# A hybrid decoder step: the next chunk's gate products ahead of the down products, and a decode maximum that reads PSUM

## The chip, the cores and the metric

The kernel runs on one core of one Trainium2 chip. The metric is the device time of one execution, in microseconds (us). A core has TensorE (PE; its weight loads are shown as PEld), VectorE (DVE), ScalarE (ACT), GpSimd (POOL) and SyncE (SP), each with an instruction queue of its own, and 16 DMA engines that move data between the chip's main memory and its working memory (SBUF). Products of TensorE land in PSUM, eight banks of 512 float32 values per partition.

## The reference

One layer of a decoder serves 512 prompt tokens and 8 samples of 4 new tokens each, 544 tokens in all, with shared weights. The width is 1024.

```python
h = h + 0.5 * rmsnorm(swiglu(rmsnorm(h, norm_g[0]), wg[0], wu[0], wd[0]), norm_g[1])
m, c_kv, k_r, s_fin = mixer(rmsnorm(h, norm_g[2]), ...)
h = h + rmsnorm(m, norm_g[3])
h = h + 0.5 * rmsnorm(swiglu(rmsnorm(h, norm_g[4]), wg[1], wu[1], wd[1]), norm_g[5])
```

`swiglu(x)` is `(silu(x @ wg) * (x @ wu)) @ wd`, with 2816 inner columns, which the kernel walks as 22 tiles of 128. The mixer has two groups of heads: a gated linear recurrence, and latent attention with a softmax over keys. For the samples the keys are 4096 cached rows each, gathered through a page table (256 latent and 64 rotary values per row). For every sample the attention computes

```python
s = (ql . c_kv + qr . k_rope) * scale       # 4 heads x 4 tokens = 16 rows against the keys
p = softmax(s);  o = p . c_kv
```

All data are float32. A product of two float32 operands is split into a high and a low part each and takes three TensorE products (high x high, high x low, low x high).

## The kernel before, in words

**Stages.** First the first FFN on all tokens (to about 390 us), then the mixer's projections, the recurrence and the prompt's attention (to about 700 us). Then two pieces of work run side by side: the samples' attention, called decode, and the second FFN on the first 256 prompt tokens (half 0). Then the output projection and the second FFN for the other 288 tokens (half 1) close the run.

**The FFN** is the generator `ffn` (line 324). Its 22 inner tiles are cut in chunks, `FCH[1]` = 6, 6, 5 and 5 tiles. For each tile f it loads the gate weight, multiplies (`gemm_q`, line 269, for half 0; `gemm` for half 1), loads the up weight, multiplies, and then scales the gate product by the row norm `r2` (line 350), forms its sigmoid in three ScalarE instructions (`sigmoid`, line 319), multiplies twice on VectorE (lines 352 and 353), and splits the result in a high part `hh` (ScalarE) and a low part `hl` (VectorE) (`split`, line 169). At the end of a chunk eight down products over the chunk's tiles follow. With `fine` the first two of them are `gemm_2` (line 280): both first take all but the chunk's last tile, and the last tile's products come at the end. `fine` is set only for the second FFN on half 0.

`weight` (line 232) loads a weight through SP's queue into one of five buffers `wraw`, casts it to the high part `wh` on ScalarE (line 250) and subtracts for the low part `wl` on VectorE (line 251).

**Quanta.** With `fine` the generator yields after every four of a product's eight inner slices, that is after 12 TensorE products of 256 columns, and after each down product (18 or 15 products). One such piece is called a quantum here.

**Decode** works on 16 halves (8 samples, two halves of 2048 keys each), class `Half`. It proceeds in steps `st` = 0 to 4 for each n. In the steps of one n, four halves are at work at different places:

- `turn`: VectorE transposes gathered keys to `kh` (line 1367), two instructions a step.
- `score` (line 1370): 80 small float32 products into two PSUM banks `self.s[0]` and `self.s[1]`, 48 of them at st = 2 and 32 at st = 4 (`RUNS`); the trace shows each as two records, 96 and 64. After the last, ScalarE copies the first bank and VectorE the second to `self.e` in SBUF (line 1385), and one VectorE reduction gives the maximum per row (`self.mx`, tile mxh, line 1387).
- `peak` (line 1389), at st = `PEAK` = 1 of the next n: a product with the identity turns and spreads the maximum (tile pm, line 1391), VectorE reduces it per query (line 1393) and forms the bias (line 1396), ScalarE takes the exponentials of `self.e` in place with their sum (line 1397), VectorE transposes them (line 1399), and 12 ScalarE and 4 VectorE copies spread them in `pbuf` (line 1403).
- `value` (line 1405), at st = 4 of that n: 16 products with the gathered rows, 32 records.
- `gathered` (line 1417), at st = 1 one n later: the output is turned and copied.

The two score banks have the tag "ps" with two buffers, so the next half's first scores wait until both are free.

**Order.** The main loop takes one decode step, and then as many quanta of the FFN's generator as keep 100 of them spread evenly over 94 steps. Each engine's instructions are put in order ahead of the run by the framework's planner: the order of the program is the priority, and an instruction that is not ready by the planner's own estimates lets later ones pass. So the order on an engine is near the program's, and not the same everywhere. `tc.issue_after` holds some instructions behind a named one; the change touches none of these. Waits between engines follow from the data and the buffers.

Of the kernel before, what the change touches and what calls it, by code (L numbers as in the profile page):

```python
# [8 lines left out]
F32 = mybir.dt.float32  # L9
# [8 lines left out]
P = 128  # L18
# [45 lines left out]
NDEC = 100  # L64
JS = ((8, 9), (0, 1), (2, 3), (4, 5), (6, 7))
KHB = 4
PEAK = 1
RUNS = {2: (0, 1, 2), 4: (3, 4)}
LEVELS = (32, 16, 8, 4, 2, 1)
CH = 64  # L70
# [40 lines left out]
def hybrid_step_kernel(  # L111
# [150 lines left out]
    def gemm(wt, act_):  # L262
        wh, wl, kt = wt
        acc = ps("acc", "acc")
        n = act_[0].shape[-1]
        mm3(acc[:, :n], [((wh[:, k], wl[:, k]), (act_[0][:, k], act_[1][:, k])) for k in range(kt)])
        return acc[:, :n]

    def gemm_q(wt, act_, step=2):
        wh, wl, kt = wt  # L270
        acc = ps("acc", "acc")
        n = act_[0].shape[-1]
        for k in range(kt):
            if k and k % step == 0:
                yield
            for i, (a, b) in enumerate(((wh, act_[0]), (wh, act_[1]), (wl, act_[0]))):
                nc.tensor.matmul(acc[:, :n], a[:, k], b[:, k], start=k + i == 0, stop=k == kt - 1 and i == 2)  # L277
        return acc[:, :n]
# [14 lines left out]
    def wcols(w, k0, kt, c0):  # L293
        return w[c0 // P, :, k0 : k0 + kt]
# [29 lines left out]
    def ffn(i, n_post, xs, u, nxt=None, mid=None, late=None, fin=None, pre=(), fine=False):  # L324
        pool = cur[-1]
        yield
        r2 = {x: u[x][2] for x in xs}
        mT = {x: actslot("m", x) for x in xs}
        ends = []
        for c, (f0, nf) in enumerate(FCH[i]):  # L330
            hh = {x: mk([P, FCH[i][0][1], HS[x]], F32R, "hh" + "ab"[x], pool=pool) for x in xs}
            hl = {x: mk([P, FCH[i][0][1], HS[x]], F32R, "hl" + "ab"[x], pool=pool) for x in xs}
            for j in range(nf):
                f = f0 + j
                wg_ = (w0 or [weight([wcols(w_g[i], 0, KD, f * P)], KD)]).pop(0)
                ga, up = {}, {}
                for x in xs:
                    ga[x] = (yield from gemm_q(wg_, u[x], 4)) if fine else gemm(wg_, u[x])
                if fine:
                    yield  # L340
                if late and f == 0:
                    behind[0] = late()
                wu_ = (w0 or [weight([wcols(w_u[i], 0, KD, f * P)], KD)]).pop(0)
                for x in xs:
                    up[x] = (yield from gemm_q(wu_, u[x], 4)) if fine else gemm(wu_, u[x])
                behind[1] = behind[0] if f == 1 else None
                for x in xs:
                    s = tmp("sil", HS[x], 3, pool)
                    t = tmp("sit", HS[x], 2, pool)
                    nc.vector.tensor_tensor(s, ga[x], r2[x], op=ALU.mult)  # L350
                    sigmoid(t, s)
                    nc.vector.tensor_tensor(s, s, t, op=ALU.mult)
                    nc.vector.tensor_tensor(s, s, up[x], op=ALU.mult)
                    split(hh[x][:, j], hl[x][:, j], s)
                yield
            last = c == len(FCH[i]) - 1
            if fin and c == BEG:
                fin.begin(u[xs[0]][2])
            if last:
                sacc = {x: tmp("ssm" + "ab"[x], HS[x], 1, pool) for x in xs}  # L360
            groups = [(d,) for d in range(KD)] if not last or len(xs) == 1 else [(d,) for d in range(KD - STAG)] + [tuple(range(KD - STAG, KD))]
            for grp in groups:
                if fine and not last and grp[0] == 0:
                    accs = yield from gemm_2([weight([wcols(w_d[i], f0, nf, d * P)], nf) for d in (0, 1)], (hh[xs[0]], hl[xs[0]]))
                elif fine and not last and grp[0] == 1:
                    accs = accs[1:]
                else:
                    accs = None
                wts = None if accs else {d: pre.pop(0) if pre else weight([wcols(w_d[i], f0, nf, d * P)], nf, len(grp) > 1) for d in grp}
                for x in xs:  # L370
                    for d in grp:
                        acc = accs[0] if accs else gemm(wts[d], (hh[x], hl[x]))
                        if last and fin and d == KD - 1:
                            fin.sums(sacc[x])
                        if c == 0:
                            nc.scalar.copy(mT[x][:, d], acc)
                        else:
                            nc.vector.tensor_tensor(mT[x][:, d], mT[x][:, d], acc, op=ALU.add)
                        if last:
                            sq = scale_sq(sacc[x], mT[x], d, gq, n_post, bool(fin) and d == KD - 1)  # L380
                        if last and fin and LAG <= d:
                            fin.column(mT[x], d - LAG)
                    if last and grp is groups[-1] and fin:
                        with tc.issue_after(fin.scale(sq).ins):
                            for d in range(KD - LAG, KD):
                                fin.column(mT[x], d)
                        fin.end(mT[x])
                    elif last and grp is groups[-1]:
                        ends.append(post(x, mT[x], sacc[x], u[x][2], nxt))
                        next(ends[-1])  # L390
                if not accs or grp[0] == 0:
                    yield
        if mid:
            mid()
        for p in ends:
            for _ in p:
                pass
# [890 lines left out]
    with scope("dec"):  # L1288
# [49 lines left out]
        class Half:  # L1338
# [31 lines left out]
            def score(self, st):  # L1370
                q = qbd[self.b % 2]
                if st == 0:
                    self.s = [ps("s", own=True) for _ in range(2)]
                for jj, j in enumerate(JS[st]):
                    for c in range(4):
                        for r in range(2):
                            rs = slice(r * 64, r * 64 + 64)
                            kh = self.kh[st][rs, c // 2, c % 2 * 4 : c % 2 * 4 + 4, jj]
                            nc.tensor.matmul(self.s[r][c * 32 : c * 32 + 32, :P], q[rs, j], kh, start=st + jj == 0, stop=st == len(JS) - 1 and jj == 1, skip_group_check=True)  # L1379
                if st == 1 and self.i and self.b + 1 < NB:  # L1380
                    qsplit(self.b + 1)
                if st < len(JS) - 1:
                    return
                for r in range(2):
                    (nc.vector.tensor_copy if r else nc.scalar.copy)(self.e[:, r * P : r * P + P], self.s[r][:, :P])
                self.mx = mk([P, 1], F32, "mxh", 2)
                nc.vector.tensor_reduce(self.mx, self.e, axis=AX.X, op=ALU.max)

            def peak(self):
                pm = ps("pm", "pm")[:, :P]  # L1390
                nc.tensor.matmul(pm, self.mx.broadcast_to([P, P]), ident, start=True, stop=True, skip_group_check=True)
                m = m3[:, self.i, self.bs]
                nc.vector.tensor_reduce(m, pm.rearrange("p (g q) -> p q g", q=16), axis=AX.X, op=ALU.max)
                mq = mk([P, 16], F32, "mq", 2)
                mb = mk([P, 1], F32, "mbd", 2)
                nc.vector.scalar_tensor_tensor(mq, m, -SCALE, selL, op0=ALU.mult, op1=ALU.mult, accum_out=mb)
                nc.scalar.activation(self.e, self.e, AF.Exp, scale=SCALE, bias=mb, accum_out=Lc[:, self.i, 0, self.b : self.b + 1])
                pt = mk([P, ROWS, 32], F32, "pt", 2)
                nc.vector.transpose(pt.rearrange("p a k -> p (a k)"), self.e)
                for c in range(4):  # L1400
                    for g in range(4):
                        src = pt[c * 32 : c * 32 + 32, g // 2 * 4 : g // 2 * 4 + 4, g % 2 * 16 : g % 2 * 16 + 16]
                        (nc.scalar.copy if g else nc.vector.tensor_copy)(self.p[g * 32 : g * 32 + 32, c // 2, c % 2 * 4 : c % 2 * 4 + 4, self.i * 16 : self.i * 16 + 16], src)  # L1403
# [62 lines left out]
        def decode_end():  # L1466
# [4 lines left out]
            for j in range(2):  # L1471
                nc.sync.dma_start(uvf[:, j], w_kv[j * P : (j + 1) * P].rearrange("p (h c) -> p h c", h=NH)[:, :, P:])
            Ll = mk([P, 2, NB], F32, "Ll")
            nc.vector.tensor_copy(Ll, Lc[:, :, 0])
            Ls = dq[:, 0, 640:896].rearrange("p (i b q) -> p i b q", i=2, b=NB)
            for i in range(2):
                nc.vector.tensor_tensor(Ls[:, i], Ll[:, i, :, None].broadcast_to([P, NB, 16]), selL[:, None, :].broadcast_to([P, NB, 16]), op=ALU.mult)
# [217 lines left out]
```

## Time and profile before

| | us |
|---|---|
| median of 3 runs | 1246.73 |
| the three runs | 1246.73, 1246.70, 1249.99 |
| profiled execution | 1247.86 |
| its span, first to last instruction | 1246.1 |
| TensorE busy in the span | 1217.1 |
| VectorE, ScalarE busy | 982.3, 739.7 |
| granted TensorE clock, mean | 0.996 |

The span lies within the profiled execution's time. Busy time counts the records of an engine; products overlap in TensorE's pipeline, so its busy time says where it has work and not how fast. A row of the profile's groups gives line, engine, operation, tiles (written <- read) with their shapes and count, then busy time in us, the mean of one in ns, and the idle time of the engine before them with what ended it. In rows of a timeline the first two numbers are the start and the duration in us, with idle time before it and its cause in square brackets. Tile names can be those of a buffer: the scores' copy `self.e` shows as q, which is a large tile that several small ones share.

### The profile page before, as it was taken

The page shows a single profiled execution, that of the slowest core. Times are in us where ns is not written, and L with a number is a line of the kernel's source. Part 1 is how long each engine was busy: PE and PEld are TensorE (multiplying, and loading weights), DVE is VectorE, ACT ScalarE, POOL GpSimd, SP SyncE. Part 2 cuts the span into 40 slices and gives each one's busy share as a digit, 9 for nine tenths or more (in the row PEclk, how much of TensorE's full clock was granted, in tenths as well). Part 3 has the DMA queues.
Part 4 walks back from the last instruction along what each step waited for, and adds up shares of the span by engine and source line. Part 5 has one row for each costly group of instructions (what it writes and reads, how often), then busy time and mean ns, then how long its engine had stood idle before and what let it go on. Part 6 is the DMA issues. An engine that isn't in the chain of part 4 may idle for free.

```text
span 1246.1 us, 30001 instructions
## 1 busy us (share of the span) xinstructions
PE 1217.1 (98%) x12366; PEld 1153.4 (93%) x12366; DVE 982.3 (79%) x1976; ACT 739.7 (59%) x1559; POOL 75.4 (6%) x80
## 2 busy tenths in 40 slices
PE   8999999999999999999999999999999999999997
PEld 6999999999999989988898888888888999999997
DVE  7897788878678888776877899999997778566665
ACT  7675545444466745445758756665656776554455
POOL 0000000000000000000001222322310000000000
PEclk9999999999999999999999999999999999999999
DMA  6232333233164223324234859878786635545551
GB/s 238 85 118 87 102 103 102 86 102 98 52 228 141 79 62 97 103 79 133 82 103 156 333 171 342 294 267 317 251 287 223 190 112 183 190 136 183 150 154 60
DMA packets 73113, 195.59 MB, mean 157 GB/s; under 512 B 12336, under 2 KB 27728, under 8 KB 68240
## 3 DMA queue, kind: packets, MB, share of 16 engines
q1 hardware_dynamic: 64512, 150.47, 37.1%
q0 software_dynamic: 7168, 41.95, 9.1%
q8 instruction: 97, 1.59, 0.5%
q10 hardware_dynamic: 1296, 1.26, 0.3%
q14 instruction: 40, 0.33, 0.1%
HBM read 183.97 MB, written 9.67 MB: 155 GB/s over the span
## 4 chain that ended last, share of the span: by engine, by line
PE 79%; DVE 9%; ACT 8%; issue 2%; DMA 1%; SPq 0%; DVEq 0%; ACTq 0%
PE acc L259 29%; PE acc L277 14%; PE dn L259 8%; PE Y L561 7%; PE X L561 4%; PE Z L561 4%; PE acc L717 3%; DVE wl L251 2%; DVE kh L1367 2%; ACT pbuf L1403 2%; ACT wh L250 2%; PE s L1379 1%; PE pa L938 1%; PE s L1188 1%; PE o L1412 1%
## 5 line engine op out<-in xcount | busy, mean ns | idle before, releaser
L250 ACT CAST wh<-wraw 128x1024 fp32r<-128x1024 f32 (+2 forms) x194 | 184.9, 957 | 159.3 <-PE acc L259 110.4
L251 DVE TENSOR_TENSOR wl<-wraw,wh 128x1024 fp32r<-128x1024 f32 (+2 forms) x194 | 214.3, 1107 | 68.6 <-ACT wh L250 68.0
L277 PE MATMUL acc<-uha,wh 128*128 128x256 f32 (+1 forms) x528 | 155.9, 296 | 0.0
L277 PE MATMUL acc<-uha,wl 128*128 128x256 f32 (+1 forms) x528 | 151.0, 287 | 0.5 <-DVE wl L251 0.4
L277 PE MATMUL acc<-ula,wh 128*128 128x256 f32 (+1 forms) x528 | 151.4, 287 | 0.0
L259 PE MATMUL acc<-uhb,wh 128*128 128x288 f32 (+1 forms) x432 | 128.1, 297 | 0.0
L259 PE MATMUL acc<-uhb,wl 128*128 128x288 f32 (+1 forms) x432 | 127.1, 295 | 1.0 <-DVE wl L251 0.7
L259 PE MATMUL acc<-ulb,wh 128*128 128x288 f32 (+1 forms) x432 | 127.7, 296 | 0.0
L277 PEld LDWEIGHTS acc<-uha,wh 128*128 128x128 f32 x528 | 99.8, 189 | 7.9 <-issue 7.3
L277 PEld LDWEIGHTS acc<-uha,wl 128*128 128x128 f32 x528 | 99.9, 190 | 2.4 <-DVE wl L251 1.7
L277 PEld LDWEIGHTS acc<-ula,wh 128*128 128x128 f32 x528 | 100.2, 190 | 1.4 <-issue 1.2
L259 PEld LDWEIGHTS acc<-uhb,wl 128*128 128x128 f32 x432 | 81.3, 188 | 1.6 <-DVE wl L251 1.6
L259 PEld LDWEIGHTS acc<-uhb,wh 128*128 128x128 f32 x432 | 81.0, 188 | 0.2 <-ACT uhb L170 0.2
L259 PEld LDWEIGHTS acc<-ulb,wh 128*128 128x128 f32 x432 | 81.1, 188 | 0.1
L259 PE MATMUL dn<-hh,dh 128*128 128x272 f32 x256 | 74.4, 291 | 0.0
L259 PE MATMUL dn<-hh,dl 128*128 128x272 f32 x256 | 73.8, 288 | 0.0
L259 PE MATMUL dn<-hl,dh 128*128 128x272 f32 x256 | 73.7, 288 | 0.0
L277 PE MATMUL acc<-uhb,wh 128*128 128x272 f32 x176 | 52.9, 300 | 0.0
L259 PE MATMUL acc<-hlb,wh 128*128 128x288 f32 x176 | 52.2, 298 | 0.0
L259 PE MATMUL acc<-hhb,wh 128*128 128x288 f32 x176 | 51.8, 298 | 0.0
L259 PE MATMUL acc<-hhb,wl 128*128 128x288 f32 x176 | 51.5, 295 | 0.0
L277 PE MATMUL acc<-uhb,wl 128*128 128x272 f32 x176 | 51.1, 290 | 0.0
(632 smaller groups left out, 3876.0 us busy)
## 6 DMA issues: line engine op xcount, KB each, us to landing
wraw<-w_u SPq DMA_DIRECT2D x66, 512.0 KB, 4.1
wraw<-w_g SPq DMA_DIRECT2D x65, 512.0 KB, 3.6
wraw<-w_d SPq DMA_DIRECT2D x40, 384.0 KB, 3.4
wraw<-w_in SPq DMA_DIRECT2D x24, 512.0 KB, 3.8
wraw<-w_d SPq DMA_DIRECT2D x32, 320.0 KB, 3.1
wraw<-w_d SPq DMA_DIRECT2D x16, 512.0 KB, 3.7
wraw<-w_o SPq DMA_DIRECT2D x16, 512.0 KB, 3.8
g_S<-state SPq DMA_DIRECT2D x4, 512.0 KB, 4.8
```

The lines of the kernel that those rows point to most:

```text
L250: nc.scalar.copy(wh[:, :kt], w[:, :kt])
L251: nc.vector.tensor_tensor(wl[:, :kt], w[:, :kt], f32(wh[:, :kt]), op=ALU.subtract)
L259: nc.tensor.matmul(out, a, b, start=n == 0, stop=n == last)
L277: nc.tensor.matmul(acc[:, :n], a[:, k], b[:, k], start=k + i == 0, stop=k == kt - 1 and i == 2)
L561: nc.tensor.matmul(bank, a[p][:, k], b[q][:, k], start=first and k + n == 0, stop=k == 3 and n == 2, skip_group_check=True)
L717: nc.tensor.matmul(accs[x, d], wts[d][p][:, k], hs[k // 2][q][:, k % 2, x], start=k + n == 0, stop=k == nf - 1 and n == 2)
L938: nc.tensor.matmul(po[es, c].rearrange("p (n m) -> p n m", m=m), kx[:, cs], up(qx[:, cs], m), start=True, stop=True, skip_group_check=True)
L1188: nc.tensor.matmul(s[:, :N], a_, b_, start=n == 0, stop=False, skip_group_check=True)
L1367: nc.vector.transpose(kh[:, g].rearrange("p a j k -> p a (j k)"), src)
L1379: nc.tensor.matmul(self.s[r][c * 32 : c * 32 + 32, :P], q[rs, j], kh, start=st + jj == 0, stop=st == len(JS) - 1 and jj == 1, skip_group_c ...
L1403: (nc.scalar.copy if g else nc.vector.tensor_copy)(self.p[g * 32 : g * 32 + 32, c // 2, c % 2 * 4 : c % 2 * 4 + 4, self.i * 16 : self.i * ...
L1412: nc.tensor.matmul(o[g : g + 32, :R], self.p[:, c, a], self.craw[c][:, a], start=i + c == 0 and a < 4, stop=i + c == 2 and a >= 4, skip_gr ...
```

## The change

Three edits.

1. In `ffn`, the gate product gets a function of its own, `gate(f)`, and the scaling, sigmoid and product with it one of its own, `swish`. With `fine`, `swish` is issued directly after the gate product, ahead of the up weight's load; and at the end of each chunk but the last, the next chunk's first `gate` (weight load, products, `swish`) is issued ahead of the chunk's down products. Without `fine` the order is as before.
2. In decode, the two copies of the scores to SBUF are gone. Two VectorE reductions read a PSUM bank each, and a small VectorE maximum joins them. Two exponentials, one for each bank, read PSUM, write `self.e`, and leave two sums, which are added at the end of decode.
3. `PEAK` is 0 instead of 1: `peak` is issued at st = 0.

```diff
-PEAK = 1
+PEAK = 0
...
+        def swish(x, z):
+            s = tmp("sil", HS[x], 3, pool)
+            t = tmp("sit", HS[x], 2, pool)
+            nc.vector.tensor_tensor(s, z, r2[x], op=ALU.mult)
+            sigmoid(t, s)
+            nc.vector.tensor_tensor(s, s, t, op=ALU.mult)
+            return s
+
+        def gate(f):
+            w = (w0 or [weight([wcols(w_g[i], 0, KD, f * P)], KD)]).pop(0)
+            z = {}
+            for x in xs:
+                z[x] = (yield from gemm_q(w, u[x], 4)) if fine else gemm(w, u[x])
+            if fine:
+                yield
+            if late and f == 0:
+                behind[0] = late()
+            return {x: swish(x, z[x]) for x in xs} if fine else z
...
-                wg_ = (w0 or [weight([wcols(w_g[i], 0, KD, f * P)], KD)]).pop(0)
-                ga, up = {}, {}
-                for x in xs:
-                    ga[x] = (yield from gemm_q(wg_, u[x], 4)) if fine else gemm(wg_, u[x])
-                if fine:
-                    yield
-                if late and f == 0:
-                    behind[0] = late()
+                up = {}
+                sg = ahead if ahead else (yield from gate(f))
+                ahead = None
                 wu_ = (w0 or [weight([wcols(w_u[i], 0, KD, f * P)], KD)]).pop(0)
...
                 for x in xs:
-                    s = tmp("sil", HS[x], 3, pool)
-                    t = tmp("sit", HS[x], 2, pool)
-                    nc.vector.tensor_tensor(s, ga[x], r2[x], op=ALU.mult)
-                    sigmoid(t, s)
-                    nc.vector.tensor_tensor(s, s, t, op=ALU.mult)
+                    s = sg[x] if fine else swish(x, sg[x])
                     nc.vector.tensor_tensor(s, s, up[x], op=ALU.mult)
                     split(hh[x][:, j], hl[x][:, j], s)
                 yield
             last = c == len(FCH[i]) - 1
+            if fine and not last:
+                ahead = yield from gate(f0 + nf)
...
+                self.mx = mk([P, 1], F32, "mxh", 2)
+                m2 = mk([P, 2], F32, "mxr", 2)
                 for r in range(2):
-                    (nc.vector.tensor_copy if r else nc.scalar.copy)(self.e[:, r * P : r * P + P], self.s[r][:, :P])
-                self.mx = mk([P, 1], F32, "mxh", 2)
-                nc.vector.tensor_reduce(self.mx, self.e, axis=AX.X, op=ALU.max)
+                    nc.vector.tensor_reduce(m2[:, r : r + 1], self.s[r][:, :P], axis=AX.X, op=ALU.max)
+                nc.vector.tensor_tensor(self.mx, m2[:, :1], m2[:, 1:], op=ALU.max)
...
-                nc.scalar.activation(self.e, self.e, AF.Exp, scale=SCALE, bias=mb, accum_out=Lc[:, self.i, 0, self.b : self.b + 1])
+                for r in range(2):
+                    nc.scalar.activation(self.e[:, r * P : r * P + P], self.s[r][:, :P], AF.Exp, scale=SCALE, bias=mb, accum_out=Lc[:, self.i, r, self.b : self.b + 1])
...
-            nc.vector.tensor_copy(Ll, Lc[:, :, 0])
+            nc.vector.tensor_tensor(Ll, Lc[:, :, 0], Lc[:, :, 1], op=ALU.add)
```

More of the change, by code (lines that the diff above doesn't have):

```diff
@@ L334, in ffn @@
                 f = f0 + j
-                wg_ = (w0 or [weight([wcols(w_g[i], 0, KD, f * P)], KD)]).pop(0)
-                ga, up = {}, {}
-                for x in xs:
-                    ga[x] = (yield from gemm_q(wg_, u[x], 4)) if fine else gemm(wg_, u[x])
-                if fine:
-                    yield
-                if late and f == 0:
-                    behind[0] = late()
+                up = {}
+                sg = ahead if ahead else (yield from gate(f))
+                ahead = None
                 wu_ = (w0 or [weight([wcols(w_u[i], 0, KD, f * P)], KD)]).pop(0)
```

## The prediction

> **What bounds the kernel now.** I read the page's busy shares first, then its chain of waits, then the stretch that the change touches by windows, then who waits for whom in it.
>
> ```profile
> span 1246.1 us, 30001 instructions
> PE 1217.1 (98%) x12366; PEld 1153.4 (93%) x12366; DVE 982.3 (79%) x1976; ACT 739.7 (59%) x1559; POOL 75.4 (6%) x80
> ...
> PE 79%; DVE 9%; ACT 8%; issue 2%; DMA 1%; SPq 0%; DVEq 0%; ACTq 0%
> ```
>
> TensorE has work 98% of the time. No product is added or removed, so the only time to win or lose is TensorE's idle time, and of that only what lies where decode runs among one FFN's products, about 700 to 960 us. The next view gives the three stretches of it that are filled with gate and up products, and the sum over all of it: start and end, length, then busy time (and instructions) of PE, PEld, DVE, ACT and POOL, the granted clock, DMA share and GB/s.
>
> ```profile
> 700.00:747.00 47.00, 46.45 (x641) 41.93 (x641) 44.77 (x92) 28.49 (x64) 12.86 (x11) 0.98 0.69 241
> ...
> 777.00:837.00 60.00, 57.93 (x1169) 50.52 (x1168) 54.32 (x123) 37.95 (x103) 17.47 (x16) 1.00 0.79 288
> ...
> 865.00:914.00 49.00, 47.06 (x928) 41.39 (x927) 44.78 (x105) 31.65 (x90) 13.33 (x12) 1.00 0.79 281
> sum 260.00, PE 252.46 PEld 221.80 DVE 237.95 ACT 161.97 POOL 62.00; mean PE 36.07 PEld 31.69 DVE 33.99 ACT 23.14 POOL 8.86
> ```
>
> TensorE is idle 260.0 - 252.5 = 7.5 us here, about 0.6% of the span. VectorE is busy 237.95 of 260, 92%: it has hardly any reserve, so what waits for VectorE waits for a queue. ScalarE, at 62%, has room. The clock is whole, so it plays no part. The idle time by cause (waiter, releaser, us in total, times, longest) in 705 to 958 us, of TensorE, of its weight loads, and of VectorE:
>
> ```profile
> PE pm L1391 <- DVE mxh L1387: 3.9, 6, 1.1
> PE acc L288 <- ACT hha L170: 1.1, 1, 1.1
> PE acc L288 <- DVE hla L171: 0.7, 1, 0.7
> ...
> PEld pm L1391 <- DVE mxh L1387: 1.9, 3, 0.8
> PEld o L1412 <- ACT pbuf L1403: 1.4, 3, 0.6
> PEld acc L288 <- ACT hha L170: 1.3, 1, 1.3
> PEld acc L288 <- DVE hla L171: 1.2, 2, 0.9
> ...
> DVE sil L352 <- ACT sit L322: 5.7, 8, 1.1
> ```
>
> The largest wait is that of the maximum's broadcast (pm, line 1391) for the maximum itself (mxh, line 1387), in nine of 16 halves. Next are the first down products (L288), which wait for the split of the last gated tile. The change touches both, in opposite directions.
>
> **The change, part by part.** First the moved gate products, at the three chunk ends of this FFN that aren't its last. Each moves one weight load of 512 KB on SP's queue ahead of eight down loads, one 1.05 us cast on ScalarE and one 1.2 us subtraction on VectorE with it, and 24 products that stand between the last up product and the first down product. Twelve of them take about 1.5 us (788.55 to 790.07 us), so 24 give the last tile some 3 us more. The longest wait there is 1.3 us. So the L288 waits go: 1.1 + 0.7 = 1.8 us by TensorE's rows, 2.5 us by its loads' rows; I take **-2.2 us**. The weights are as many as before and the ring of five is the same, so I cost the moved load at nothing; uncovered it would cost its landing, 3.6 us by the page, three times.
>
> Second, the sigmoid chain. In this FFN the scaling, sigmoid and product with it are issued after the gate product instead of after the up product, and the same instructions run. The row of 5.7 us says that VectorE stands still for it eight times. Issued sooner, it can as well stand in front of something that was ready: bounds -5.7 and +5.7 us. What idles VectorE reaches TensorE only in the part of the stretch where VectorE lags; I take **-1.0 us**.
>
> Third, the maximum. These are the groups whose work goes, and the nearest for what comes (busy us, mean ns):
>
> ```profile
> L1385 DVE COPY q<-s 128x128 f32<-128x128 f32 x16 | 4.1, 254 | 0.0
> L1385 ACT COPY q<-s 128x128 f32<-128x128 f32 x16 | 4.1, 257 | 0.4 <-PE s L1379 0.3
> L1387 DVE TENSOR_REDUCE mxh<-q 128x1 f32<-128x256 f32 x16 | 6.1, 382 | 0.1
> L1397 ACT ACTIVATE q<-q,mbd 128x256 f32<-128x256 f32 x16 | 8.2, 510 | 14.5 <-DVE mq L1396 14.1
> L1397 ACT ACTIVATION_READ_ACCUMULATOR q<-q,mbd 128x1 f32 x16 | 3.0, 186 | 0.0
> ...
> L1195 DVE TENSOR_REDUCE mx<-s 128x1 f32<-128x256 f32 x4 | 1.7, 416 | 0.0
> L1195 DVE TENSOR_REDUCE mx<-s 128x1 f32<-128x128 f32 x4 | 1.1, 283 | 0.0
> L1196 DVE TENSOR_SCALAR mx<-mx 128x1 f32<-128x1 f32 x16 | 2.3, 147 | 0.0
> L1199 ACT ACTIVATE pe<-s,mx 128x128 f32<-128x128 f32 x4 | 1.5, 367 | 2.6 <-DVE mx L1196 2.1 <-ACT pe L1199 0.5
> ```
>
> The prompt's attention reads its scores from PSUM in just these shapes. VectorE per half: two reductions and a small one, 2 x 283 + 147 = 713 ns, for 254 + 382 = 636 ns: +0.077 us, 1.2 us over 16 halves. ScalarE: 2 x (367 + 186) = 1106 for 257 + 510 + 186 = 953 ns: +0.15 us, 2.4 us in all, under ScalarE's 38% of free time. "No copies" is thus no less work on either engine. I charge VectorE's share where it lags, **+0.5 us** (0 to 1.2).
>
> The Trainium skill, "VectorE: DVE Perf Modes", section "Rules for kernel authors", says of elementwise work on a matmul output that one accepts the slow rate from PSUM, or copies to SBUF first if many operations follow. The rows show a smaller gap: a 256-wide maximum takes 416 ns from PSUM and 382 from SBUF, so the copy of 254 ns bought 34; by the rule the sum would be no better than mine, by the rows it is the 0.5 us above.
>
> Fourth, the place of the broadcast, one decode step sooner. A step carries about one quantum of FFN work, 12 products. One half, PE first, then VectorE, then ScalarE:
>
> ```profile
> 785.60 1.16 PE L1379 MATMUL s<-kh,q 64*32 64x128 f32 x64
> 788.55 0.39 PE L277 MATMUL acc<-uha,wh 128*128 128x256 f32 x1
> 790.07 0.28 PE L277 MATMUL acc<-uha,wh 128*128 128x256 f32 x1
> 791.95 0.46 PE L1391 MATMUL pm<-ident,mxh 128*128 128x128 f32 x2 [0.30 <-DVE mxh L1387]
> 794.22 1.05 PE L1379 MATMUL s<-kh,q 64*32 64x128 f32 x56
> ...
> 787.96 1.21 DVE L251 TENSOR_TENSOR wl<-wraw,wh 128x1024 fp32r<-128x1024 f32 x1
> 789.09 0.41 DVE L171 TENSOR_TENSOR hla<-sil,hha 128x256 fp32r<-128x256 f32 x1
> 789.42 0.70 DVE L1367 STREAM_TRANSPOSE kh<-hb 128x512 f32<-128x512 f32 x1
> ...
> 790.64 0.25 DVE L1385 COPY q<-s 128x128 f32<-128x128 f32 x1
> 790.82 0.69 DVE L1367 STREAM_TRANSPOSE kh<-hb 128x512 f32<-128x512 f32 x1
> 791.43 0.38 DVE L1387 TENSOR_REDUCE mxh<-q 128x1 f32<-128x256 f32 x1
> ...
> 794.32 0.51 ACT L1397 ACTIVATE q<-q,mbd 128x256 f32<-128x256 f32 x1
> ```
>
> The scores end at 786.76, but VectorE comes to the copy only at 790.64, 3.9 us later: it isn't waiting, it works off a weight's subtraction, a split and transposes that stand ahead in its queue. The maximum is there at 791.81 and the broadcast starts at once; it sets the start. One quantum sooner the broadcast stands at 790.07, and TensorE waits 1.7 us there, 1.4 more than now. That cost is paid once per stretch in which VectorE lags, since while TensorE stands still VectorE works off its queue and the lag is smaller at the next half. Three stretches of gate and up products make 3 x 1.4 = 4.2 us. Against it the maximum may be sooner: from copy to the reduction's end are 1.17 us now; rows of one queue overlap by some 0.07 us (790.64 + 0.25 against 790.82), so two reductions and the small one take about 0.6, or 1.2 with a transpose put between, as now. I take half of the difference, 0.3 us, off each: 4.2 - 0.9 = **+3.3 us**. Bounds: -5.8 (all of 3.9 + 1.9 goes) and 9 x 1.4 = +12.6.
>
> Fifth, the end of decode. The values' three waits for pbuf (1.4 us) are all of the last half, behind which no decode work stands:
>
> ```profile
> 953.73 0.21 PEld L1412 LDWEIGHTS o<-ha,pbuf 128*32 128x32 f32 x8 [0.22 <-ACT pbuf L1403]
> 955.27 0.16 PEld L1412 LDWEIGHTS o<-hb,pbuf 128*32 128x32 f32 x8 [0.61 <-ACT pbuf L1403]
> ```
>
> A step sooner the copies to pbuf come about one quantum sooner, which is more than the wait: **-1.0 us** (0 to -1.4). The waits behind the moved instructions are in ScalarE's queue: the weight casts behind two exponentials. They had 38% slack.
>
> Sum: -2.2 - 1.0 + 0.5 + 3.3 - 1.0 = -0.4 us. The profiled execution took 1247.86 us, 1.8 more than its span; the runs' median is 1246.73, 1.1 lower. Taken off the median: **1246.3 us**, no change that can be measured.
>
> **The rivals.** *Faster.* If the planned order lets VectorE reach the reductions with less queued ahead, the broadcast costs nothing, the sigmoid's stalls go by half (-2.9), the L288 waits by the loads' count (-2.5) and the end by 1.4, with 0.5 charged: -6.3, 1240.4 us. For it: VectorE's waits are for ScalarE's chain, which is issued sooner. Against: VectorE's work isn't less.
>
> *Slower, the maximum late in every half.* The nine halves that wait today each pay 1.4 us more: +12.6 - 2.2 - 1.0 + 0.5 - 1.0 = +8.9, 1255.6 us. It decides when VectorE comes to the reductions more than about 2.6 us after the scores' end (790.07 less 0.7 less 786.76). For it: 3.9 us above. Against: it needs VectorE's work to be tied so closely to TensorE's that a stop of TensorE frees nothing.
>
> *Slower, the banks held.* The next scores may not start before the exponentials have read these. Today they may: 794.22 against an exponential's end at 794.83. The worst half:
>
> ```profile
> 746.39 0.38 PE L1391 MATMUL pm<-ident,mxh 128*128 128x128 f32 x2
> 750.76 0.51 ACT L1397 ACTIVATE q<-q,mbd 128x256 f32<-128x256 f32 x1 [0.73 <-DVE mq L1396]
> ```
>
> From broadcast to the exponential's end are 4.9 us here and 2.9 in the half above; two exponentials add 0.3. Two quanta of about 1.5 us and the broadcast's 0.3 lie between: 3.3. So a half pays from nothing (3.2) to 1.9 us (5.2); the mean, 0.95, in seven lagging halves makes 6.7 - 0.4 = +6.3: 1253.0 us. Against: with the broadcast a step sooner fewer VectorE instructions are queued between. The Trainium skill, "PSUM — Partial Sum Buffer", section "Summary: rules for kernel authors", advises to evacuate promptly; it would speak for this rival, and the row of 794.22 agrees that the bank is wanted again at once.
>
> *It doesn't do what it says.* The scores of one step already stand split among products in places; if the planner puts the broadcast behind the same 24 products, the third part's cost goes and the gain is 2.2 + 1.0 + 1.0 - 0.5: 1243.0 us, at the edge of no change.
>
> **How the numbers follow.** Forecast 0.34; faster 0.31; maximum late 0.16; banks held 0.11; broadcast not moved 0.08. About 0.3% (3.7 us) is what can be told from no change. The last rival is put half to the same and half to faster: faster 0.35, same 0.38, slower 0.27. The range reaches a little past both sides, 1239 to 1256 us.
>
> **What would show it.** Right: no wait at L288, broadcast waits that are about as long in total as today's 5.8 us but lie at the first halves of each stretch, no wait of the score products for ScalarE. Wrong: broadcast waits over 10 us; score products waiting for the exponentials; VectorE's idle time for the sigmoid doubled; a changed time outside 700 to 960 us.

## The result, and the profile after

| | before | changed |
|---|---|---|
| median, us | 1246.87 | 1257.70 (six runs, 1255.55 to 1263.22) |
| ratio to before | | 1.0085, 95% interval 1.0071 to 1.0099 |
| profiled execution, its span | 1247.86, 1246.1 | 1257.54, 1255.8 |
| granted clock of that execution | 0.996 | 0.993 |

Three executions of the experiments below took 1.3 to 1.9 times as long as the others of their kernel; all medians and ratios leave them out.

The change makes the kernel slower by 10.8 us. The forecast was no change, and the time lies just beyond the upper end of the range. The page of the changed kernel shows no other bound: its lines for the span, the busy shares and the chain's shares are

```profile
span 1255.8 us, 30041 instructions
PE 1221.5 (97%) x12366; PEld 1158.7 (92%) x12366; DVE 982.0 (78%) x1992; ACT 739.7 (59%) x1575; POOL 75.7 (6%) x80
...
PE 81%; DVE 9%; ACT 7%; issue 2%; DMA 1%; DVEq 0%; SPq 0%; ACTq 0%
```

The products are as many, and VectorE is busy as long (982.0 against 982.3 us). The windows over decode, in the columns of the prediction's, show where the time is:

```profile
700.00:747.00 47.00, 43.78 (x622) 38.90 (x621) 44.79 (x94) 28.36 (x63) 13.07 (x11) 1.00 0.71 251
747.00:777.00 30.00, 30.00 (x545) 26.74 (x544) 27.30 (x63) 18.74 (x55) 7.60 (x8) 0.95 0.80 293
777.00:837.00 60.00, 54.91 (x1029) 48.60 (x1032) 50.13 (x112) 36.09 (x102) 14.18 (x14) 0.94 0.74 264
...
865.00:914.00 49.00, 45.06 (x841) 38.61 (x834) 44.23 (x101) 27.56 (x76) 14.56 (x14) 1.00 0.79 281
914.00:937.00 23.00, 23.00 (x413) 20.89 (x414) 18.79 (x49) 13.61 (x45) 2.85 (x3) 0.93 0.78 260
...
sum 260.00, PE 247.35 PEld 218.25 DVE 230.50 ACT 153.95 POOL 60.54; mean PE 35.34 PEld 31.18 DVE 32.93 ACT 21.99 POOL 8.65
```

TensorE's idle time went from 7.5 to 12.7 us. And in three stretches its granted clock is no longer whole: 0.95, 0.94 and 0.93 of 30, 60 and 23 us are 6.7 us of work lost. The trace's own record of the clock has four windows of 3.41 us at half clock there; that of the kernel before has one, from 698.02 us on, mostly ahead of these stretches. Over the whole span TensorE's idle time rose by 5.3 us (29.0 to 34.2) and the work lost to half clock by 4.4 us (4.4 to 8.8, the last microseconds of each span included). Together they are the 9.7 us by which the span grew. Nothing of weight lies outside decode.

The waits of the changed kernel between 705 and 975 us (waiter, releaser, us in total, times, longest), first of TensorE, then of its loads, then of VectorE:

```profile
PE pm L1406 <- DVE mxh L1402: 11.1, 6, 2.8
PE o L1436 <- ACT q L1431: 1.3, 1, 1.3
PE acc L277 <- DVE wl L251: 1.2, 2, 0.7
...
PEld pm L1406 <- DVE mxh L1402: 1.4, 2, 1.2
...
DVE hla L171 <- ACT hha L170: 4.6, 5, 1.4
DVE sil L336 <- ACT sit L322: 4.3, 7, 1.3
```

TensorE's own wait at the broadcast grew from 3.9 us to 11.1 us. The loads' rows for the broadcast (1.9 us before, 1.4 us now) aren't added to it: a weight load and its product stand still together. In the kernel before the loads at 805.41 and 893.36 us end the same stops as the products there, and the third, at 833.41 us, held its product up by 0.12 us. So the prediction's "nine of 16 halves" are seven. The first down products (L288) no longer wait, nor do the values wait for pbuf, and no score product waits for an exponential. VectorE's idle time for the sigmoid went from 5.7 to 4.3 us. The half of the prediction's example, from the timeline, PE first, then VectorE:

```profile
787.05 1.16 PE L1393 MATMUL s<-kh,q 64*32 64x128 f32 x64
...
790.00 0.39 PE L277 MATMUL acc<-uha,wh 128*128 128x256 f32 x1
...
791.41 0.28 PE L277 MATMUL acc<-uha,wl 128*128 128x256 f32 x1
793.87 0.46 PE L1406 MATMUL pm<-ident,mxh 128*128 128x128 f32 x2 [2.18 <-DVE mxh L1402]
...
789.93 1.21 DVE L251 TENSOR_TENSOR wl<-wraw,wh 128x1024 fp32r<-128x1024 f32 x1
791.06 0.41 DVE L171 TENSOR_TENSOR hla<-sil,hha 128x256 fp32r<-128x256 f32 x1
791.39 0.70 DVE L1381 STREAM_TRANSPOSE kh<-hb 128x512 f32<-128x512 f32 x1
792.02 0.67 DVE L1381 STREAM_TRANSPOSE kh<-mb 128x512 f32<-128x512 f32 x1
792.62 0.45 DVE L1401 TENSOR_REDUCE mxr<-s 128x1 f32<-128x128 f32 x2
792.99 0.69 DVE L1381 STREAM_TRANSPOSE kh<-hb 128x512 f32<-128x512 f32 x1
793.61 0.12 DVE L1402 TENSOR_TENSOR mxh<-mxr 128x1 f32<-128x1 f32 x1
```

The broadcast does stand one quantum sooner, behind 12 products instead of 24. The same work as before stands ahead of the reductions on VectorE, and a transpose still lies between them and the joined maximum. So the maximum comes 5.5 us after the scores' end (793.73 less 788.21), where it came 5.1 us after it, and TensorE stops for 2.18 us instead of 0.30.

The time to the maximum's end for four halves in a row, each worked out from the rows of one execution, in us, and counted from 0.06 us after the last score product's start, which is 0.2 us ahead of the end used above:

| half | 4 | 5 | 6 | 7 |
|---|---|---|---|---|
| before | 5.3 | 5.6 | 6.1 | 5.2 |
| changed | 5.7 | 3.2 | 6.3 | 2.7 |

A stop does let VectorE catch up, for one half. At the next half but one the lag is back whole. TensorE stops for the maximum at halves 1, 4, 6, 11, 12 and 14, for 1.9, 2.2, 2.8, 1.0, 2.8 and 0.4 us.

### The profile page after: what moved, and what is told of

It reads as the page before. It is cut to its first block, busy times and chain, and to the rows that moved or that the text cites. A ratio compares the mean times of both kernels' runs of the same rounds, so it can differ in the third digit from the quotient of the medians.

```text
span 1255.8 us, 30041 instructions
## 1 busy us (share of the span) xinstructions
PE 1221.5 (97%) x12366; PEld 1158.7 (92%) x12366; DVE 982.0 (78%) x1992; ACT 739.7 (59%) x1575; POOL 75.7 (6%) x80
## 4 chain that ended last, share of the span: by engine, by line
PE 81%; DVE 9%; ACT 7%; issue 2%; DMA 1%; DVEq 0%; SPq 0%; ACTq 0%
PE acc L259 30%; PE acc L277 15%; PE dn L259 8%; PE Y L575 6%; PE X L575 4%; PE Z L575 4%; DVE kh L1381 3%; PE acc L731 3%; DVE wl L251 2%; PE s L1393 2%; ACT pbuf L1419 2%; ACT wh L250 1%; PE o L1428 1%; PE pa L952 1%; PE s L1202 1%
```

## The experiments

Three theories. *Late maximum*: TensorE pays at the sooner place what VectorE lags. *Held banks*: it pays because the next scores wait for the exponentials. *FFN order*: the moved gate products do it. Later ones are told where they come up. All times are medians; the kernel before took 1247.6 us beside the first four runs and 1247.4 beside the next four.

**The parts apart.** The changed kernel with the broadcast in its old place:

```diff
-PEAK = 0
+PEAK = 1
```

> The changed kernel with the broadcast of the maximum back at its old place (PEAK = 1); the rest of the change stays. Late maximum (the sooner broadcast stands in TensorE's queue before VectorE has the maximum): the cost goes with the place, so 1242 to 1246 us, broadcast waits at most 5 us. Held banks (the next scores wait for exponentials that read PSUM): the later broadcast makes it worse, 1256 us or more, and the score products wait for ScalarE for 5 us or more. FFN order (the early sigmoid chain and the moved gate products load VectorE where it lags): still 1252 us or more, with neither wait grown.

The FFN part alone, with decode as before (copies, one exponential, PEAK = 1):

> The FFN's part of the change alone; decode as before. Late maximum and held banks both: 1243 to 1246 us, since only the waits of the first down products go, about 2 us, and broadcast waits stay near 5.8 us. FFN order: 1252 us or more.

The decode part alone, with `ffn` as before:

> Decode's part alone (maximum and exponentials read PSUM, broadcast one step sooner); FFN as before. Late maximum: 1256 to 1261 us, broadcast waits 10 us or more, no score product waiting for ScalarE. Held banks: as slow, but score products wait for ScalarE by 5 us or more. FFN order: 1246 to 1249 us.

And of the whole change only PEAK = 0, in the kernel before:

> The kernel before with the broadcast one step sooner and nothing else; the scores are still copied out of PSUM, so no bank is held. Late maximum: 1253 to 1258 us, broadcast waits 10 us or more. Held banks and FFN order: 1246 to 1249 us.

| | broadcast in its old place | one step sooner |
|---|---|---|
| FFN before, copies | 1247.57 | 1263.23, ratio 1.0125 (1.0108 to 1.0143) |
| FFN before, PSUM read | not run | 1258.75, ratio 1.0085 (1.0072 to 1.0098) |
| FFN changed, copies | 1244.94, ratio 0.998 (0.9972 to 0.9989) | below, on another chip |
| FFN changed, PSUM read | 1252.14, ratio 1.0034 (1.0022 to 1.0046) | 1257.70, ratio 1.0085 (above) |

The row of TensorE that grew most, or the one of the broadcast, of each of the four between 690 and 990 us, in the order of the runs:

```profile
PE s L1393 <- ACT q L1413: 7.3, 5, 2.7
```

```profile
PE pm L1405 <- DVE mxh L1401: 2.7, 2, 1.4
```

```profile
PE pm L1392 <- DVE mxh L1388: 11.9, 8, 2.8
```

```profile
PE pm L1391 <- DVE mxh L1387: 12.8, 9, 2.9
```

The FFN part is a gain of 2.6 us. The sooner place alone costs 15.7 us, all the loss and more. Reading PSUM has no one price: with the broadcast sooner it saves 4.5 us (1263.23 to 1258.75, with the FFN before), and with the broadcast in its old place it costs 7.2 (1244.94 to 1252.14, with the FFN changed). There it is the banks that are held: the score products wait 7.3 us for the exponentials and the broadcast for nothing. The sooner place alone cost more than *Late maximum* expected (1253 to 1258 us), and 1252.14 us lies between what *Late maximum* and *Held banks* expected. By the waits and the FFN part's gain, *FFN order* is out, *Late maximum* holds for the change as it is, and *Held banks* for the change without the sooner place.

**Is it the clock?** The changed kernel, with 14 products into unused columns of the broadcast's bank ahead of it at the four halves with the longest stops:

```diff
+                if self.n in (1, 4, 6, 12):
+                    for _ in range(14):
+                        nc.tensor.matmul(pb[:, 256:512], u4[0][0][:, 1, :P], u4[0][0][:, 0], start=True, stop=True, skip_group_check=True)
```

> The changed kernel, with 14 products that nobody reads (128x256, about 118 ns each, 1.65 us) put directly ahead of the maximum's broadcast at the four halves whose stop was 1.9 us or more (k1, k4, k6, k12). They take up part of the waiting time, so TensorE stands still for 0.2 to 1.3 us there instead of 2.0 to 3.0; the maximum comes as late as before. Theory Clock (a stop of 1.9 us or more is followed by 3.41 us at half rate, which costs 1.7 us each time): the four dips go, 1257.7 - 4 x 1.7 = about 1251, between 1249 and 1253, granted clock back at 0.998 or more. Theory Stops alone (the halved clock is hidden by waits, or is there whatever TensorE does): no change, 1256.5 to 1258.5.

1262.47 us: neither. Behind these four stops the clock stays whole, but the edit moved more than the stops. The planner put a weight's subtraction ahead of the broadcast's reduction, as VectorE's timeline at half 4 shows, the sigmoid went ahead of the exponential on ScalarE, and score products now wait, with one window of half clock behind that wait:

```profile
799.64 0.38 DVE L334 TENSOR_TENSOR sil<-acc,rna 128x256 f32<-128x256 f32 x1
799.95 1.20 DVE L251 TENSOR_TENSOR wl<-wraw,wh 128x1024 fp32r<-128x1024 f32 x1
801.08 0.28 DVE L1412 TENSOR_REDUCE q<-pm 128x16 f32<-128x128 f32 x1
```

The waits of TensorE in the same kernel:

```profile
PE pm L1410 <- DVE mxh L1402: 8.4, 7, 2.2
...
PE s L1393 <- ACT q L1417: 1.7, 1, 1.7
```

As a test of the clock it is inconclusive. The six runs of the changed kernel say more: the one with a granted clock of 0.999 over the whole span took 1255.55 us, the one with 0.997 took 1256.02, the three with 0.993 or 0.994 took 1257.54 to 1258.19, the one with 0.990 took 1263.22. With hardly any half clock the kernel is still 8.7 us slower than the median of before. So the half clock is worth some 2 us of the median's 10.8, as an estimate from these few runs; that the rest of its loss is given back, because VectorE catches up meanwhile, is argued and not shown.

**The FFN part's halves, and two ways to a better kernel.** All three start from the FFN part alone. Both score copies on ScalarE:

```diff
-                    (nc.vector.tensor_copy if r else nc.scalar.copy)(self.e[:, r * P : r * P + P], self.s[r][:, :P])
+                    nc.scalar.copy(self.e[:, r * P : r * P + P], self.s[r][:, :P])
```

> The kernel with the FFN part alone (decode as in the kernel before), with both copies of a half's scores on ScalarE instead of one on each engine. VectorE gets 0.254 us per half less, ahead of the maximum's reduction. Theory VectorE's queue (the maximum is late for what stands ahead of it on VectorE): the two waits of the broadcast (2.7 us in all) shrink by some 0.25 us per waiting half, more if the relief adds up over halves: 1242.5 to 1244.5 against 1244.9. Theory ScalarE: two copies in a row on ScalarE make the reduction start 0.25 us later than it did and nothing is won: 1244.9 to 1246.5.

Without the next chunk's gate products ahead, so that only the sooner sigmoid is left:

> The kernel with the FFN part alone, without the gate products ahead of the down products: only the sooner scaling and sigmoid is left. It sizes the two halves of the FFN part, which together made 1244.9 against 1247.6 before. If the moved gate products bring it (the waits at the first down products, put at 2.2 us): about 1247, with these waits back. If the sooner sigmoid brings it: about 1245, and the first down products don't wait much either.

PEAK = 2, the broadcast a step later than before:

> The kernel with the FFN part alone and the maximum's broadcast one decode step later than before instead of one sooner. Theory Late maximum (each half costs what VectorE lags behind the broadcast's place): no broadcast waits are left, 2.7 us less: 1242 to 1244. Theory of a new wait: the exponentials and pbuf's copies come some 1.5 us later and the values wait for pbuf, or the next scores share the broadcast's step: 1245 to 1250, with waits for pbuf in the trace.

They took 1243.65 us (ratio 0.9968, 0.9955 to 0.998), 1247.83 (1.0004, 0.9996 to 1.0013) and 1273.02 (1.0203, 1.0189 to 1.0218). The sooner sigmoid alone is worth nothing that can be told; the gate products ahead bring the FFN part's gain, about 3 us, and without them the L288 row of 1.1 us is back. VectorE relieved of a 0.25 us copy per half gives the lowest median of the study, ahead of both kernels of the case; its interval doesn't tell it from the FFN part alone (0.998). A step later no broadcast waits, but the values do, since pbuf is late. The row is of the weight loads; TensorE's own rows for these waits are 10.5 and 4.9 us:

```profile
PEld o L1426 <- ACT pbuf L1417: 47.8, 63, 3.1
```

The old place is thus near the best one: a step sooner the maximum is late, a step later pbuf.

**Does the price come from VectorE's load?** First the split's subtraction went to GpSimd, in the changed kernel, in the fastest one, and in that with PEAK = 0:

```diff
-                    split(hh[x][:, j], hl[x][:, j], s)
+                    split(hh[x][:, j], hl[x][:, j], s, nc.gpsimd if fine else None)
```

> The changed kernel, with the subtraction of the split in this FFN (hla, 0.41 us per gate tile) moved from VectorE to GpSimd, so that VectorE has some 15 x 0.4 = 6 us less between 700 and 960 us while the broadcast keeps its sooner place. Theory VectorE's lag (the sooner broadcast costs because VectorE comes late to the reductions): the broadcast's waits, 12.5 us in the changed kernel, fall by half or more; 1249 to 1253 instead of 1257.7. Theory Place (a broadcast in that place costs some 10 us whatever VectorE has to do): 1256 to 1259 with the waits as before. If GpSimd's subtraction is slow, waits of the down products for it appear at L288.

> The kernel with the FFN part alone and both copies on ScalarE (1243.65), with the same subtraction on GpSimd. Theory VectorE's lag: the last broadcast waits (1.6 us) go: 1241 to 1243. If TensorE is the bound by now, no change: 1243.2 to 1244.2. If GpSimd's subtraction is slow or late: 1244.5 to 1250, with waits at the first down products.

> The kernel of the run above with the broadcast one decode step sooner, as in the change, copies kept on ScalarE. Theory VectorE's lag: with VectorE relieved the sooner place costs some 3 to 6 us where it cost 15.7 with the kernel before: 1244 to 1249. Theory Place: the same 15 us: 1256 to 1260.

These three fell on a chip on which the kernel before took 1254.11 us, so only ratios are compared: 1.0034 (1.0021 to 1.0047), 0.9999 (0.999 to 1.0008) and 1.0007 (0.9999 to 1.0016). The sooner place costs 0.08% there instead of 1.25%, as *VectorE's lag* has it. But the 1.25% is of the kernel before, with its FFN order and its copies; the subtraction takes 1.0 us on GpSimd; and score products pause in these traces at "issue" by 3.1 to 4.1 us, where no trace from the first chips has more than 0.7. So load and chip aren't told apart. A wait and a group of the changed kernel with the subtraction on GpSimd:

```profile
PE s L1393 <- issue: 4.1, 13, 0.6
```

```profile
L171 POOL TENSOR_TENSOR hla<-sil,hha 128x256 fp32r<-128x256 f32 x21 | 21.3, 1016 | 114.4 <-ACT hha L170 114.3
```

So the relief was made without GpSimd, by leaving the low part of the split out (the down products read the high part in its place, as many products as before), and its controls were run on the same chip. The edit also drops a tile, which can move the planner's order; no run separates that:

```diff
-            hl = {x: mk([P, FCH[i][0][1], HS[x]], F32R, "hl" + "ab"[x], pool=pool) for x in xs}
+            hl = hh if fine else {x: mk([P, FCH[i][0][1], HS[x]], F32R, "hl" + "ab"[x], pool=pool) for x in xs}
...
-                    split(hh[x][:, j], hl[x][:, j], s)
+                    if fine:
+                        nc.scalar.copy(hh[x][:, j], s)
+                    else:
+                        split(hh[x][:, j], hl[x][:, j], s)
```

> The kernel with the FFN part alone (ratio to before 0.998) with the broadcast one decode step sooner and the copies kept. The sooner place alone made the kernel before slower by 1.25%, 15.7 us. Theory VectorE's lag: the FFN part leaves VectorE as loaded as before, so the place costs about as much again, 12 to 16 us: ratio 1.008 to 1.011.

> The kernel with the FFN part alone; in this FFN the small half of the gated tile's split isn't computed, and the down products read the large half in its place, the same number of products. It leaves out 0.41 us of VectorE work per gated tile, some 6 us between 700 and 960 us, and adds nothing anywhere. Theory VectorE's lag: the two broadcast waits (2.7 us) go, ratio 0.995 to 0.9975. If TensorE alone sets the pace: 0.998 as without it.

> The kernel of the run above (without the small half of the split) with the broadcast one decode step sooner, copies kept. Theory VectorE's lag: with 6 us less of VectorE work the price of the sooner place falls to less than half of what it is with the FFN part alone: ratio 0.2 to 0.6% above that of the run above. Theory Place: the same 1.0 to 1.25% above it.

> The changed kernel (ratio 1.0085), without the small half of the split in this FFN, down products reading the large half. Theory VectorE's lag: broadcast waits fall from 12.5 us to 6 or less, ratio 1.000 to 1.004. Theory Place: 1.007 to 1.0085, waits as before.

> The changed kernel itself, on the same chip as the next two. Theory VectorE's lag and theory Place both: slower than before; 1.0085 on a chip on which score products never pause, less than that (1.004 to 1.007) on a chip on which they do, because the pauses of TensorE let VectorE catch up.

> The kernel with the FFN part alone, on the same chip: 0.997 to 0.9995 on either kind of chip; its difference to the run above is the price of the decode part there.

> The changed kernel without the small half of the split, on the same chip as the changed kernel itself. Theory VectorE's lag: at least half of the difference between the two runs above goes, ratio 1.000 to 1.004. Theory Place: within 0.1% of the changed kernel.

These seven ran on one chip; the kernel before took 1254.9 and 1255.0 us beside them.

| ratio to before | VectorE as it is | relieved |
|---|---|---|
| FFN part, copies, old place | 1.0017 (1.0008 to 1.0026) | 0.9979 (0.997 to 0.9988) |
| the same, a step sooner | 1.0045 (1.0029 to 1.006) | 0.9972 (0.996 to 0.9984) |
| the changed kernel | 1.0048 (1.0034 to 1.0062) | 0.9997 and 0.9998 (0.9989 to 1.0007) |

With VectorE as it is the sooner place costs 0.28%, 3.5 us, and relieved nothing (-0.07%); by the intervals each difference is certain to about 0.18%. *Place* expected the same price in both columns, so with the copies the price comes from VectorE's load. For the change itself this isn't shown: the whole decode part costs 0.31% and 0.18%, and what lies between these is within the intervals. Three expectations missed on this chip: the FFN part a step sooner was to cost 0.8 to 1.1%, the sooner place with the relief 0.2 to 0.6%, and the FFN part alone was to gain.

What the relief does to the stops is shown by TensorE's waits at the broadcast, of the changed kernel on this chip and with the relief. Each of these stops ends within 0.15 us of the maximum's end, whatever the row names:

```profile
PE pm L1406 <- DVE mxh L1402: 5.2, 4, 2.2
...
PE pm L1406 <- DVE mxr L1401: 2.6, 1, 2.6
...
PE pm L1406 <- PE acc L277: 2.1, 1, 2.1
```

```profile
PE pm L1409 <- DVE mxh L1405: 4.3, 5, 2.0
...
PE pm L1409 <- remote: 1.8, 1, 1.8
```

They fall from 9.9 to 6.1 us. At half 6 the maximum comes 6.1 us after the scores in the changed kernel on this chip, and 2.8 us with the relief; at half 4 it gains little (5.7 and 5.4), and at half 7 it comes later (2.7 and 4.5). With the copies the stops fall only from 5.8 to 4.9 us, but the longest falls from 2.9 to 1.6, and two half-clock windows between 700 and 960 us go. These are single executions. What the relief brings in the old place, 0.38%, where no row shows a wait of the broadcast, isn't explained by that.

On this chip the change costs 0.48% where it cost 0.85%, and the FFN part loses instead of gaining. The rows of the score products, of the changed kernel and of the FFN part alone:

```profile
PE s L1393 <- issue: 3.1, 8, 0.7
```

```profile
PE s L1393 <- issue: 8.2, 20, 2.2
```

TensorE's pauses there are time in which VectorE can catch up, which would fit a smaller price; no run tests it. What the pauses are is open.

## Why the prediction was wrong

Its sum was -0.4 us. Term by term:

- *The waits at L288, -2.2*: right. The rows are gone, and on the first chips the FFN part gained 2.6 us, by the runs nearly all of it from the moved gate products.
- *The sigmoid, -1.0*: too much; alone it made +0.04%, within its interval of nothing. VectorE's idle time for it fell only from 5.7 to 4.3 us.
- *VectorE's and ScalarE's work, +0.5*: right as work, for the rows of the changed kernel give VectorE 2 x 267 + 126 = 660 ns a half against 636, and ScalarE 2 x (361 + 196) = 1114 against 953:

```profile
L1401 DVE TENSOR_REDUCE mxr<-s 128x1 f32<-128x128 f32 x32 | 7.3, 267 | 0.3 <-PE s L1393 0.3
...
L1402 DVE TENSOR_TENSOR mxh<-mxr 128x1 f32<-128x1 f32 x16 | 2.0, 126 | 0.0
...
L1413 ACT ACTIVATE q<-s,mbd 128x128 f32<-128x128 f32 x32 | 11.4, 361 | 9.7 <-DVE mq L1411 9.7
L1413 ACT ACTIVATION_READ_ACCUMULATOR q<-s,mbd 128x1 f32 x32 | 6.3, 196 | 0.0
```

  What it missed is that this edit and the place depend on one another: -4.5 us at the sooner place, +7.2 at the old one. The Trainium skill's advice in "PSUM — Partial Sum Buffer", section "Summary: rules for kernel authors", to evacuate promptly, is borne out by the second number and not by the first.
- *The sooner broadcast, +3.3*: this is the step that failed, in two places. "That cost is paid once per stretch in which VectorE lags" took the relief of a stop to last, and it lasts for one half: the lag falls from 5.7 to 3.2 us behind a stop and stands at 6.3 at the half after. So two of the three stretches pay twice (halves 4 and 6, 11 and 12). That VectorE has too little free time, 8% in the kernel before, to work its queue off for longer fits this, but no run shows it alone. And the price of one stop, 1.4 us less the 0.3 us by which "the maximum may be sooner", was too low: at half 4 the maximum came 0.5 us later instead, and the stops at halves 4, 6 and 12 are 1.9, 1.7 and 1.7 us longer than before. In all TensorE's waits at the broadcast rose by 7.2 us instead of 3.3, and the longer stops cost clock as well.
- *The clock, nothing*: "The clock is whole, so it plays no part" was read from the windows of before, whose first row has 0.98. It was true of before's other stretches and not of a kernel with longer stops: four half-clock windows, at most 4 x 1.7 = 6.8 us of work lost, and some 2 us of the median by the runs.
- *The end of decode, -1.0*: right in that the rows of pbuf are gone; behind them the product that turns the output (L1436) now waits 1.3 us for ScalarE where it waited 0.9, so part of it is lost again.

Of the rivals, *the maximum late in every half* came nearest in time (1255.6) and named the mechanism, with its point of decision: 5.5 us is far more than 2.6. It isn't every half, and the price of each is higher: nine stops of 1.4 us and no clock were summed, where six stops and four half-clock windows came, so that the time is so near is partly luck. *The banks held*, priced at 6.7 us, is near in size (7.2 us measured) but belongs to the kernel in which the broadcast isn't sooner; there five waits of up to 2.7 us make it, not seven of 0.95, so the sizes agree by luck. Here no score product waits for an exponential. The signs were named well: broadcast waits over 10 us were the first sign of "wrong", and TensorE's own row has 11.1.

## What to carry to other kernels

Before a consumer is moved ahead on a full engine, measure how late its producer is, half by half, and price every half that lags; here a stop cleared the lag of an engine that is busy 92% of the time, but only for one half. A copy out of PSUM that looks like waste can be what frees the bank: weigh it together with the place of its reader, for the two have a joint price. And on a TensorE that is nearly always busy, ask of each stop whether it is long enough to cost clock as well.

## What the runs showed of the hardware

**In decode, stops of about half of 3.41 us were followed by half clock.** Windows of 3.41 us of the changed kernel, laid around the stop at half 4:

```profile
787.64:791.05 3.41, 3.41 (x80) 2.29 (x65) 3.41 (x6) 0.68 (x2) 2.24 (x3) 1.00 0.60 210
791.05:794.46 3.41, 1.23 (x11) 1.06 (x10) 3.41 (x10) 1.04 (x1) 1.87 (x2) 1.00 0.91 280
794.46:797.87 3.41, 3.41 (x18) 3.41 (x18) 2.50 (x9) 3.07 (x12) 0.00 (x0) 0.50 1.01 413
797.87:801.28 3.41, 3.41 (x112) 3.08 (x112) 2.69 (x8) 3.22 (x10) 0.00 (x0) 1.00 0.81 315
```

TensorE is idle for 2.18 us of the second window, and the third is granted half the clock: products of 118 ns take 213. The half-clock windows of this execution start at 746.67, 794.46, 825.18 and 913.93 us, which are 14, 9 and 26 times 3.413 us apart. So the grid runs by itself in these traces. Between 700 and 960 us, over all traces of this study, what counted is TensorE's idle time within one of its windows: all 26 windows with 1.71 us or more were followed by half clock, one of the three with 1.67 to 1.70 us was, and none with under 1.6 us. So the same stop can cost clock in one execution and not in another: it can lie in one window or across two. Idle time as the profile shows it isn't the whole rule. Near 694 us, among other products, windows with only 0.7 us of idle time were followed by half clock in six traces, the kernel before among them (694.61 us, 0.73 us), and the half clock from 693.68 us of the kernel with the 14 products lasted for three windows with TensorE busy in the last two. What the gate counts there is open. The Trainium skill, "TensorE: Matmul & The Clock Gate", section "What's actually happening", has a free-running window of 3413 ns, and the trace agrees. The same page of the Trainium skill, section "Why this matters for your kernels", asks for no gaps above about 3 us; there the trace differs, and the measurement decides: half a window of idle time was enough.

**Chips differ by 0.6%.** The kernel before took 1246.9 to 1247.6 us beside the runs on some chips and 1254.1 to 1255.0 beside those on two others. In the traces of altered kernels from the latter, runs of many small products pause at "issue", by 1.5 to 8.2 us in all; the kernel before was not profiled there, and what the products wait for isn't in the profile.
